# A recurrence's step products in one TensorE form, and its score loads by halves in other gaps

## The chip, the cores and the metric

One core of a Trainium2 chip runs the whole kernel as one program. The metric is the device time of one execution in microseconds (us). PE is TensorE (matrix products, with PEld for its weight loads), DVE is VectorE, ACT is ScalarE, POOL is GpSimd and SP is SyncE, which only issues DMAs here.

## The reference

A decoder trunk of two layers over 16 meta tokens and 1024 tokens of width 1024. The first layer mixes by the RWKV-7 recurrence, the second by stick-breaking attention; each is followed by a conv-gated MLP. The change lies in the first layer's recurrence alone:

```
def step(S, inp):                       # per head, S is 64 x 64, 16 heads, 1040 tokens
    r_t, w_t, k_t, v_t, a_t, b_t = inp  # a_t = -kk, b_t = kk * a, w_t = decay
    sa = jnp.einsum('bhij,bhj->bhi', S, a_t)
    S = (S * w_t[:, :, None, :] + sa[..., None] * b_t[:, :, None, :]
         + v_t[..., None] * k_t[:, :, None, :])
    return S, jnp.einsum('bhij,bhj->bhi', S, r_t)
_, y = lax.scan(step, S0, seq)
...                                     # then a group norm of y per head, a bonus, a gate and w_o
```

## The kernel before

The projections of the first layer are written to DRAM per segment of 512 tokens (two segments, s) and per four heads (four groups, q), scaled by the running products of the decay. `rwkv_chain` then runs the recurrence in chunks of 64 tokens. A unit is one (q, s): four heads, as two pairs u with two heads e each, over eight chunks. There are eight units, one after the other; before them stands a prelude that loads and prepares the first ones and does the 16 meta tokens (`first_chunk`).

`stage_c` is the serial part. For each chunk c (a step) it makes c1 = AR x S0 (tile c), adds KV and gets R (on DVE), makes c2 = XT x R (tiles c and c2b), copies it to UV (DVE and ACT), makes c3 = BKt x UV (tile c again) and from it the next state S, and makes the output yp from UV x Ar and S0 x AR. Between these products stand three gaps per step, 24 in a unit. I call gap c.k the gap behind the first (k = 0), second (1) and last products (2) of step c. What fills a gap is written out by hand in the table `SEQ`, one string of letters per gap. Each letter pulls a generator one step:

- A (`stage_a`, two units ahead): loads BK and AR, then makes the scores A, which go masked to Aa, and writes them to DRAM as AD. B (`stage_b`): the second half of the scores, Ar.
- L and S (`stage_s`, two units ahead) and s (one unit ahead): load AT, which is AD spread to four copies, 1 MB; copy XL; then 31 steps of forward substitution, two POOL instructions each (prd = AT x XL, XL += prd); at the end XL is written to DRAM as XD.
- x and X (`stage_x`, one ahead): load X11t from XD, transpose it on DVE to X, and make XT by two rounds of small products G.
- V, T (one ahead): v and BK transposed by TensorE (vt, kv, bt). F (one back): the norm of y: products hr_gn and hp_gn, on POOL y x G and later y + B, then the store of y to DRAM.

`PRE` is the like table of the prelude. The engines DVE, POOL and SP run these instructions in the order in which they are written (`InOrder`), TensorE as well (`pmm`). So a wait of one instruction holds all that are behind it on its engine, and a DMA that waits on SP holds the DMAs behind it.

AR is zero in the rows of the other head: AR[es, u, e] is loaded for es alone and the rest is cleared once. UV and BKt are laid out by head in the same way. In the form names of the profile, 128*64 is a product with 128 rows of contraction and 64 columns of weights, 64*64 one with 64 and 64.

Of the kernel before, what the change touches and what calls it, by code (L numbers as in the profile page):

```python
# [9 lines left out]
F32 = mybir.dt.float32  # L10
F32R = mybir.dt.float32r
AF = mybir.ActivationFunctionType
ALU = mybir.AluOpType
# [3 lines left out]
P = 128  # L17
# [34 lines left out]
def kernel(ctx: ExitStack, tc: tile.TileContext, a: dict, out: bass.AP):  # L52
# [142 lines left out]
    NC = 8  # L195
# [586 lines left out]
    def rwkv_chain(late, early, last):  # L782
# [13 lines left out]
        def pmm(*args, **kw):  # L796
            return tc.keep_in_program_order(mm(*args, **kw))  # L797

        def ptr(*args):
# [8 lines left out]
            g=16, S=128, R=128, PS=128, y=1024, GB=1024, ysq=1024, XT=1024, Ar=2048, UV=2048, BKt=2048, KV=1024, AR=4096,  # L808
# [21 lines left out]
        selw = rp.tile([P, 64], F32, name="selw")  # L830
# [54 lines left out]
        def norm_out(nm, y, nt, per, G1, B1, dst):  # L885
# [8 lines left out]
            for i in range(nt):  # L894
                pmm(ps[:, 64 * i : 64 * i + 64], ysq[:, i * P : (i + 1) * P], selw, start=True, stop=True)
                if i == 3:
                    yield
# [3 lines left out]
                xs.rearrange("p (i e) -> p i e", e=2), ps.rearrange("p (i x) -> p i x", x=64)[:, 0:nt, 0:2],  # L901
# [190 lines left out]
        def stage_a(q, s, ed):  # L1092
            nm = f"{q}{s}"
            AR = ARs[(4 * s + q) % 3]
            BK = [place(f"BK{'ab'[u]}{q % 2}", f"BK{u}_{nm}") for u in range(2)]
            for u in range(2):
                LQ.dma_start(BK[u], BK_s[s][q][:, u, 0:1024])
                for e in range(2):
                    es = slice(64 * e, 64 * e + 64)
                    LQ.dma_start(AR[es, u, e, :], AR_s[s][q][es, u, 0:1024])  # L1100
            ed.update(AR=AR, BK=BK)
            yield
            Aa = place(f"Aa{q % 2}", f"Aa{nm}").rearrange("p (u c e t) -> p u c e t", u=2, c=NC, e=2)
            ed["Aa"] = Aa

            AD = dr.tile([4, NC, 32, 2, 32], F32, tag="AD", bufs=2, name=f"AD{nm}")
            for u in range(2):
                yield from chunk_mats(nm, BK, AR, 0, Aa, u)
                flush(evacs)
                for b4 in range(4):  # L1110
                    e, b = b4 // 2, b4 % 2
                    LQ.dma_start(
                        AD[b4][:, :, u, :].rearrange("c j t -> j c t"),
                        Aa[32 * b4 : 32 * b4 + 32, u, :, e, 32 * b : 32 * b + 32],
                    )
            ed["AD"] = AD
            yield

        def stage_s(q, s, ed):
            nm = f"{q}{s}"  # L1120
            AD = ed["AD"]
            AT = place(f"AT{q % 2}", f"AT{nm}").rearrange("p (j u t) -> p j u t", j=32, u=2)
            LQ.dma_start(
                AT.rearrange("p j u t -> p (j u t)"),
                AD.rearrange("q c j u t -> (q c) (j u t)").unsqueeze(0).broadcast_to([4, 32, 2048]),
            )
            yield
# [112 lines left out]
        def stage_c(q, s, ed, gap):  # L1240
# [3 lines left out]
            for c in range(NC):  # L1244
# [3 lines left out]
                R = place(f"R{c % 2}", f"R{nm}{c}").rearrange("p (u d) -> p u d", u=2)  # L1248
                PS0 = place(f"PS{c % 2}", f"PS{nm}{c}").rearrange("p (u d) -> p u d", u=2)
                c1 = ps_c(f"c1{nm}{c}")  # L1250
                for u in range(2):
                    for e in range(2):
                        es = slice(64 * e, 64 * e + 64)
                        pmm(c1[es, u * 64 : u * 64 + 64], arv[es, u, e, c, 0, :], S0[es, u, :], start=True, stop=True)
                gap()
                V.tensor_tensor(R, c1[:, 0:128].rearrange("p (u d) -> p u d", u=2), KV[:, :, c, :], op=ALU.add)
# [4 lines left out]
                for u in range(2):  # L1261
                    for e in range(2):
                        us = slice(64 * e, 64 * e + 64)
                        pmm(c2[e][us, u * 64 : u * 64 + 64], XT[us, u, c, :], R[us, u, :], start=True, stop=True)
# [10 lines left out]
                yp = ps_y(f"yp{nm}{c}")  # L1275
                for u in range(2):
                    for e in range(2):
                        es = slice(64 * e, 64 * e + 64)
                        o = slice(u * 64, u * 64 + 64)
                        pmm(yp[es, o], UV[:, u, c, e, :], Ar[:, u, c, e, :], start=True, stop=False)  # L1280
                        pmm(yp[es, o], S0[es, u, :], arv[es, u, e, c, 1, :], start=False, stop=True)
# [37 lines left out]
        def gens(fn):  # L1319
# [6 lines left out]
            "A": (gA, 2), "B": (gB, 1), "L": (gS, 2), "S": (gS, 2), "s": (gS, 1), "x": (gX, 1), "X": (gX, 1),  # L1326
            "V": (gV, 1), "T": (gT, 1), "F": (gF, -1),
        }
        before = {"L": gA, "x": gS}
# [10 lines left out]
        def run(gs):  # L1340
# [6 lines left out]
            "a W2 f c2 a11 s2 A b20 a9 f v s4 t5 A t15 s2 A s2 A2 s2 A s2 A s6 A s2 A2 s2 A A s4 A s2 "  # L1347
            "A2 s A s2 A s9 A2 s2 A13 s2 A2 s4 S2 v20 f34 s30 x21 S20 W3 f "
# [3 lines left out]
            "TFAsTsss VFTTsssss Asss AFTssss AFAFssss AAssss FBsss FAssss AFss AFV LxBB V BF VF V VF SV "  # L1352
            "VBSSS VBSBSSF VBSS SXSVXBS XSSSXF XSSSS BXSSSXSFF "
# [9 lines left out]
        def clear_rest():  # L1363
            for t in ARs[1:]:
                clear(t, G)
            yield
            for t in XTs:
                G.memset(t, 0.0)
            yield
# [4 lines left out]
            "c": clear_rest(),  # L1374
# [1155 lines left out]
```

## Time and profile before

| what | value |
|---|---|
| device time, median of three runs | 3647.41 us (3642.76 to 3652.55) |
| the profiled execution's own time | 3653.89 us |
| its span, first to last instruction | 3652.2 us |
| PE busy | 3205.0 us (88%) |
| DVE, ACT, POOL busy | 2310.3, 1558.4, 1737.8 us |
| mean granted TensorE clock | 0.914 of full |

The span is what the profile covers; the time beside it also holds what lies around the first and the last instruction. A busy share is a mean over stages with different limits: the recurrence is about one seventh of the span, and only its own stretch tells what bounds it. The granted clock has two levels, 1.00 (2.4 GHz) and 0.50 (1.2 GHz). A row of the windows' view holds the stretch (us from the span's start), its length, the busy time of PE, PEld, DVE, ACT and POOL with their instructions, the granted clock, the DMA engines' busy share and GB/s. A timeline row holds the start, the time taken, engine, line, operation, output and inputs, form and count.

### The profile page before, as it was taken

The numbers are of one execution on the slowest core, as the hardware profiler recorded it, in microseconds if no ns is written. First come the engines' busy times: TensorE is split into PE (matmuls) and PEld (weight loads), VectorE is DVE, ScalarE is ACT, GpSimd is POOL, SyncE is SP. The second block draws the span as 40 slices with busy tenths as digits, with TensorE's granted clock in tenths as the row PEclk, the third lists the DMA queues.
The fourth block names the chain that finished last, engine by engine and source line by source line (L and its number), as shares of the span: only waits on it lengthen the run. The fifth ranks groups of instructions, "written<-read, shape, count | busy, mean of one in ns | idle before, by whom it ended". The sixth has DMA issues, their size and how long they took to land.

```text
span 3652.2 us, 62577 instructions
## 1 busy us (share of the span) xinstructions
PE 3205.0 (88%) x25101; PEld 2967.3 (81%) x25101; DVE 2310.3 (63%) x3064; ACT 1558.4 (43%) x2859; POOL 1737.8 (48%) x1676
## 2 busy tenths in 40 slices
PE   4798688489889979999999988888888699998998
PEld 4796466367777969999899978788878699998998
DVE  8778866423232488888734377777774888887342
ACT  4664544133344333333323266666653333334232
POOL 5555634343644465445422366666644544444221
PEclk7898799679887989999999999999999799999999
DMA  6344343443434422222445301010025222224453
GB/s 200 109 152 132 122 129 113 117 100 85 118 94 148 132 63 76 76 82 73 145 140 164 98 22 29 24 33 24 21 100 165 94 78 80 76 79 139 122 165 95
DMA packets 438398, 366.61 MB, mean 100 GB/s; under 512 B 66823, under 2 KB 359453, under 8 KB 436827
## 3 DMA queue, kind: packets, MB, share of 16 engines
q1 hardware_dynamic: 437243, 361.28, 32.8%
q8 instruction: 197, 3.23, 0.4%
q0 software_dynamic: 864, 1.33, 0.1%
q14 instruction: 94, 0.77, 0.1%
HBM read 266.51 MB, written 96.02 MB: 99 GB/s over the span
## 4 chain that ended last, share of the span: by engine, by line
PE 48%; DVE 20%; DMA 7%; ACT 6%; issue 5%; POOL 4%; SPq 1%; ACTq 0%; DVEq 0%; POOLq 0%
PE dn L1508 12%; DVE t L1691 5%; DMA XD<-XL 3%; PE yp L797 3%; PE kps L2090 2%; DVE rs L1616 2%; DVE om L2245 2%; PE c L797 1%; PE wt L2093 1%; ACT t L1689 1%; PE wo L1900 1%; PE vps L2090 1%; PE kp L217 1%; DMA araw<-a_s 1%; PE av L2090 1%
## 5 line engine op out<-in xcount | busy, mean ns | idle before, releaser
L1508 PE MATMUL dn<-act,h_dn 128*128 128x260 f32 x2688 | 437.0, 284 | 5.0 <-ACT act L76 3.3
L1508 PEld LDWEIGHTS dn<-act,h_dn 128*128 128x128 f32 x2688 | 373.2, 190 | 5.8 <-ACT act L76 3.7
L1691 DVE SCALAR_TENSOR_TENSOR t<-u,pcol,t 128x1040 f32<-128x1040 f32 x168 | 304.1, 1811 | 108.7 <-ACT t L1689 108.6
L1508 PE MATMUL dn<-act,l_dn 128*128 128x260 f32 x1344 | 273.2, 285 | 2.0 <-POOL l_dn L1457 2.0
L2248 POOL TENSOR_TENSOR be<-be,om 128x911 f32<-128x911 f32 (+7 forms) x128 | 195.7, 1529 | 130.4 <-DVE om L2245 103.6
L1457 POOL TENSOR_TENSOR l_dn<-r_dn,h_dn 128x1024 fp32r<-128x1024 f32 (+1 forms) x46 | 101.6, 2208 | 325.0 <-ACT h_dn L76 324.2
L2245 DVE TENSOR_TENSOR_SCAN om<-om 128x912 f32<-128x912 f32 (+7 forms) x128 | 215.7, 1685 | 48.2 <-POOL om L2240 30.1
L1706 POOL TENSOR_TENSOR t<-t,t 128x1040 f32<-128x1040 f32 x42 | 103.3, 2460 | 250.5 <-DVE t L1691 250.5
L76 ACT ACTIVATE h_dn<-r_dn 128x1024 fp32r<-128x1024 f32 (+1 forms) x92 | 90.7, 986 | 298.5 <-PE dn L1508 272.9
L1508 PEld LDWEIGHTS dn<-act,l_dn 128*128 128x128 f32 x1344 | 207.1, 189 | 2.4 <-POOL l_dn L1457 2.4
L44 POOL TENSOR_TENSOR prd<-AT,XL 128x108 f32<-128x108 f32 (+24 forms) x217 | 80.4, 371 | 164.5 <-DMA AT<-AD 111.6
L1457 POOL TENSOR_TENSOR s34l<-rs,s34h 128x1024 fp32r<-128x1024 f32 x44 | 105.8, 2405 | 103.2 <-ACT s34h L76 103.2
L76 ACT ACTIVATE WT<-wt 128x512 fp32r<-128x512 f32 (+2 forms) x224 | 98.7, 443 | 120.3 <-PE wt L2093 92.0
L2311 DVE TENSOR_TENSOR WT<-wt,WT 128x512 fp32r<-128x512 f32 (+2 forms) x224 | 107.6, 488 | 53.2 <-ACT WT L76 49.4
L2090 PE MATMUL av<-WT,VS 128*128 128x256 f32 (+3 forms) x640 | 108.4, 283 | 32.6 <-DVE WT L2311 32.5
L76 ACT ACTIVATE s34h<-rs 128x1024 fp32r<-128x1024 f32 x44 | 46.7, 1062 | 202.8 <-PE wo L1508 5.1
L1457 DVE TENSOR_TENSOR l_dn<-r_dn,h_dn 128x1024 fp32r<-128x1024 f32 (+1 forms) x46 | 52.0, 1131 | 123.1 <-ACT h_dn L76 123.0
L2093 PE MATMUL wt<-ident,be 128*128 128x128 f32 x576 | 99.3, 295 | 34.4 <-DVE WTm L2286 33.6
L217 PE MATMUL kp<-xm,wh_rw_wk 128*128 128x264 f32 (+1 forms) x384 | 108.3, 375 | 17.6 <-DVE xm L396 10.5
L2240 POOL TENSOR_SCALAR_AFFINE_SELECT be<-be 128x128 f32<-128x128 f32 x128 | 78.6, 614 | 91.9 <-ACT be L2235 91.9
L2090 PEld LDWEIGHTS av<-WT,VS 128*64 128x64 f32 (+1 forms) x640 | 85.5, 165 | 43.7 <-DVE WT L2311 42.5
L797 PE MATMUL A<-ARz,BK 128*128 128x128 f32 x512 | 86.7, 311 | 30.7 <-DVE prd L44 20.5
(2104 smaller groups left out, 11207.5 us busy)
## 6 DMA issues: line engine op xcount, KB each, us to landing
r_dn<-in_ffn_down_dram SPq DMA_DIRECT2D x60, 512.0 KB
a_s<-t SPq DMA_DIRECT2D x84, 260.0 KB
rv<-in_ffn_up_dram SPq DMA_DIRECT2D x42, 512.0 KB
ra<-in_ffn_up_dram SPq DMA_DIRECT2D x42, 512.0 KB
araw<-a_s SPq DMA_DIRECT2D x50, 260.0 KB
r_dn<-in_ffn_down_dram SPq DMA_DIRECT2D x32, 384.0 KB
raw<-a_s SPq DMA_DIRECT2D x36, 260.0 KB
hr<-h_s SPq DMA_DIRECT2D x32, 260.0 KB
```

Source lines behind the costliest of these rows:

```text
L76: return S.activation(o, i, AF.Copy, scale=scale)
L217: return tc.keep_in_program_order(mm(*args, **kw))
L797: return tc.keep_in_program_order(mm(*args, **kw))
L1457: eng.tensor_tensor(lo, x, f(hi), op=ALU.subtract)
L1508: self.mm(ps[:, c, :], w[:, kk, :], X[k][i][:, c * CH : (c + 1) * CH], start=k == 0 and j == 0, stop=k == len(X) - 1 and j == 2,)
L1691: VV.scalar_tensor_tensor(t[j], u[j][:, i : i + n], w, t[j], op0=ALU.mult, op1=ALU.add)
L1706: (G if n == L else VV).tensor_tensor(t[1], t[0], t[1], op=ALU.mult)
L2090: return tc.keep_in_program_order(mm(*args, **kw))
L2093: return tc.keep_in_program_order(nc.tensor.transpose(*args))
L2245: V.tensor_tensor_scan(om[0:nq, 0:nk], om[0:nq, 0:nk], om[0:nq, 0:nk], 1.0, op0=ALU.mult, op1=ALU.min)
L2248: G.tensor_tensor(be[0:nq, 1:nk], be[0:nq, 1:nk], om[0:nq, 0 : nk - 1], op=ALU.mult)
L2311: V.tensor_tensor(wt[:, 1, s0:s1], ps[:, s0:s1], f(wt[:, 0, s0:s1]), op=ALU.subtract)
```

## The change

The products c1, c2 and the second half of yp take all 128 rows instead of the 64 of their own head; for this R gets a zeroed place for the other head (`Rs`, cleared once on POOL), and its addition becomes two instructions, one per head. In yp the two heads' products follow each other, first UV x Ar for both, then S0 x AR for both. The constant selw of the norm is half as wide. `stage_a` yields between the loads of BK and of AR, writes AD by pair u, and loads AT by halves itself, one half behind each pair's scores. `stage_s` loads nothing any more. The tables put the letters into other gaps, L is gone, and a new letter P pulls `stage_a` three units ahead (its first step, the loads of BK).

```
-        selw = rp.tile([P, 64], F32, name="selw")
+        Rs = [place(f"R{i}", f"Rz{i}").rearrange("p (u e d) -> p u e d", u=2, e=2) for i in range(2)]
+
+        selw = rp.tile([P, 32], F32, name="selw")
...
             for u in range(2):
                 LQ.dma_start(BK[u], BK_s[s][q][:, u, 0:1024])
+            yield
+            for u in range(2):
                 for e in range(2):
                     es = slice(64 * e, 64 * e + 64)
                     LQ.dma_start(AR[es, u, e, :], AR_s[s][q][es, u, 0:1024])
...
-            AD = dr.tile([4, NC, 32, 2, 32], F32, tag="AD", bufs=2, name=f"AD{nm}")
+            AD = dr.tile([2, 4, NC, 32, 32], F32, tag="AD", bufs=2, name=f"AD{nm}")
+            AT = ed["AT"] = place(f"AT{q % 2}", f"AT{nm}").rearrange("p (u j t) -> p u j t", j=32, u=2)
             for u in range(2):
                 yield from chunk_mats(nm, BK, AR, 0, Aa, u)
                 flush(evacs)
                 for b4 in range(4):
                     e, b = b4 // 2, b4 % 2
                     LQ.dma_start(
-                        AD[b4][:, :, u, :].rearrange("c j t -> j c t"),
+                        AD[u][b4].rearrange("c j t -> j c t"),
                         Aa[32 * b4 : 32 * b4 + 32, u, :, e, 32 * b : 32 * b + 32],
                     )
-            ed["AD"] = AD
+                LQ.dma_start(
+                    AT[:, u].rearrange("p j t -> p (j t)"),
+                    AD[u].rearrange("q c j t -> (q c) (j t)").unsqueeze(0).broadcast_to([4, 32, 1024]),
+                )
             yield
 
         def stage_s(q, s, ed):
             nm = f"{q}{s}"
-            AD = ed["AD"]
-            AT = place(f"AT{q % 2}", f"AT{nm}").rearrange("p (j u t) -> p j u t", j=32, u=2)
-            LQ.dma_start(
-                AT.rearrange("p j u t -> p (j u t)"),
-                AD.rearrange("q c j u t -> (q c) (j u t)").unsqueeze(0).broadcast_to([4, 32, 2048]),
-            )
-            yield
+            AT = ed["AT"].rearrange("p u j t -> p j u t")
...
-                        pmm(c1[es, u * 64 : u * 64 + 64], arv[es, u, e, c, 0, :], S0[es, u, :], start=True, stop=True)
+                        pmm(c1[es, u * 64 : u * 64 + 64], arv[:, u, e, c, 0, :], S0[:, u, :], start=True, stop=True)
                 gap()
-                V.tensor_tensor(R, c1[:, 0:128].rearrange("p (u d) -> p u d", u=2), KV[:, :, c, :], op=ALU.add)
+                for e in range(2):
+                    es = slice(64 * e, 64 * e + 64)
+                    V.tensor_tensor(
+                        R[es, :, e, :], c1[es, 0:128].rearrange("p (u d) -> p u d", u=2), KV[es, :, c, :], op=ALU.add
+                    )
...
-                        pmm(c2[e][us, u * 64 : u * 64 + 64], XT[us, u, c, :], R[us, u, :], start=True, stop=True)
+                        pmm(c2[e][us, u * 64 : u * 64 + 64], XT[:, u, c, :], R[:, u, e, :], start=True, stop=True)
...
                 for u in range(2):
+                    o = slice(u * 64, u * 64 + 64)
                     for e in range(2):
-                        es = slice(64 * e, 64 * e + 64)
-                        o = slice(u * 64, u * 64 + 64)
-                        pmm(yp[es, o], UV[:, u, c, e, :], Ar[:, u, c, e, :], start=True, stop=False)
-                        pmm(yp[es, o], S0[es, u, :], arv[es, u, e, c, 1, :], start=False, stop=True)
+                        pmm(yp[64 * e : 64 * e + 64, o], UV[:, u, c, e, :], Ar[:, u, c, e, :], start=True, stop=False)
+                    for e in range(2):
+                        pmm(yp[64 * e : 64 * e + 64, o], S0[:, u, :], arv[:, u, e, c, 1, :], start=False, stop=True)
...
         SEQ = (
-            "TFAsTsss VFTTsssss Asss AFTssss AFAFssss AAssss FBsss FAssss AFss AFV LxBB V BF VF V VF SV "
-            "VBSSS VBSBSSF VBSS SXSVXBS XSSSXF XSSSS BXSSSXSFF "
+            "ATsss TVsss TTsss AAsss AAsss AAsss AAsss Asss FBsss BBsss xFV BFV "
+            "BFVS BFVSSS BFVSSS BFVSSS BFVSSS XVFSSS XFSSS XFSSS XFSSS XFSSS XFPSSS XFFSSSS "
         ).split()
```

On TensorE, this is the second half of a step in unit 3 of eight, before: c from UV and BKt is the last state product, yp the first half of the output group (its second half repeats it), in turn from Ar and UV and from AR and the state S.

```order
L797 MATMUL c_8498<-UV_7958,BKt_7716 64x64 x4
L797 MATMUL yp_8503<-Ar_7892,UV_7958 64x64
L797 MATMUL yp_8503<-ARz_5796,S_8445 64x64
L797 MATMUL yp_8503<-Ar_7892,UV_7958 64x64
L797 MATMUL yp_8503<-ARz_5796,S_8445 64x64
```

The same place of the changed kernel, with the scores A that follow in the gap:

```order
L797 MATMUL c_8494<-UV_7980,BKt_7743 64x64 x4
L797 MATMUL yp_8499<-Ar_7930,UV_7980 64x64 x2
L797 MATMUL yp_8499<-ARz_5796,S_8451 64x64 x2
L797 MATMUL yp_8499<-Ar_7930,UV_7980 64x64 x2
L797 MATMUL yp_8499<-ARz_5796,S_8451 64x64 x2
L797 MATMUL A_8513<-ARz_5798,BK_11_8345 128x128 x4
```

The eight products are the same in number; they now stand in pairs of one kind.

On SP, this is one unit's round of DMAs before, from the store of the unit's predecessor's y (y_s) to the loads of X11t; G, B and vc are inputs of the norm and of V.

```order
L44 DMA y_s_91<-y_6421 128x512
L44 DMA G_7722<-g_s_138 128x2x512
L44 DMA BK_01_7724<-BK_s_125 128x1024
L44 DMA ARz_5797<-AR_s_117 64x1024 x2
L44 DMA BK_01_7725<-BK_s_125 128x1024
L44 DMA ARz_5797<-AR_s_117 64x1024 x2
L44 DMA vc_7751<-vc_s_132 128x2x512
L44 DMA B_7756<-b_s_146 128x2x512
L44 DMA AD_7792<-Aa_7791 32x8x32 x8
L44 DMA AT_7974<-AD_7792 128x1x2048
L44 DMA XD_7983<-XL_7470 256x1x64 x4
L44 DMA X11t_7988<-XD_7983 32x8x64 x4
```

The same round of the changed kernel:

```order
L44 DMA y_s_91<-y_6435 128x512
L44 DMA BK_01_7697<-BK_s_125 128x1024
L44 DMA BK_01_7698<-BK_s_125 128x1024
L44 DMA ARz_5797<-AR_s_117 64x1024 x4
L44 DMA vc_7768<-vc_s_132 128x2x512
L44 DMA AD_7815<-Aa_7814 32x8x32 x4
L44 DMA AT_7816<-AD_7815 128x1x1024
L44 DMA AD_7815<-Aa_7814 32x8x32 x4
L44 DMA AT_7816<-AD_7815 128x1x1024
L44 DMA G_7928<-g_s_138 128x2x512
L44 DMA XD_7953<-XL_7395 256x1x64 x4
L44 DMA X11t_7969<-XD_7953 32x8x64 x4
```

AT goes out in two halves, the first between the two groups of AD writes; G and B (behind X11t) have moved back, and the store of y still stands ahead of BK and AR.

On POOL, this is where y + B stands in the substitution of one unit, before; the last number of a row counts down from 31 with the steps of the substitution.

```order
L44 TENSOR_TENSOR XL_8116<-XL_8116,prd_8155 128x4x26
L44 TENSOR_TENSOR prd_8155<-AT_7974,XL_8116 128x4x25
L44 TENSOR_TENSOR XL_8116<-XL_8116,prd_8155 128x4x25
L44 TENSOR_TENSOR y_7062<-y_7062,B_7756 128x1024
L44 TENSOR_TENSOR prd_8155<-AT_7974,XL_8116 128x4x24
```

And in the changed kernel:

```order
L44 TENSOR_TENSOR XL_8042<-XL_8042,prd_8066 128x8x19
L44 TENSOR_TENSOR prd_8066<-AT_7816,XL_8042 128x8x18
L44 TENSOR_TENSOR y_7085<-y_7085,B_7978 128x1024
L44 TENSOR_TENSOR XL_8042<-XL_8042,prd_8066 128x8x18
L44 TENSOR_TENSOR prd_8066<-AT_7816,XL_8042 128x8x17
```

It has moved from behind the fourteenth instruction of the substitution to behind the twenty-seventh.

## Rows read from the trace of the kernel before

**Rows 1.** The page's head.

```profile
span 3652.2 us, 62577 instructions
```

**Rows 2.** Windows: units 0, 6, 7, the sum of all eight, and within unit 7.

```profile
755.60:811.20 55.60, 48.92 (x613) 39.22 (x614) 15.42 (x49) 21.02 (x57) 25.42 (x67) 0.84 0.33 81
...
1099.90:1145.60 45.70, 44.52 (x608) 35.67 (x608) 13.85 (x45) 22.54 (x59) 18.39 (x39) 0.91 0.23 64
1145.60:1203.00 57.40, 53.99 (x405) 43.45 (x406) 14.23 (x43) 19.87 (x49) 20.59 (x13) 0.62 0.65 200
sum 447.40, PE 407.25 PEld 328.49 DVE 126.79 ACT 175.99 POOL 204.87; mean PE 50.91 PEld 41.06 DVE 15.85 ACT 22.00 POOL 25.61
...
1146.00:1184.00 38.00, 36.25 (x252) 29.20 (x254) 8.83 (x28) 15.28 (x36) 18.24 (x12) 0.50 0.76 236
```

**Rows 3.** Windows inside unit 3.

```profile
928.10:931.90 3.80, 3.80 (x22) 3.07 (x23) 0.57 (x2) 2.38 (x6) 3.56 (x5) 0.50 1.04 268
931.90:970.30 38.40, 37.90 (x444) 30.56 (x442) 13.42 (x40) 13.21 (x39) 12.34 (x33) 1.00 0.29 73
970.30:975.80 5.50, 0.02 (x1) 0.00 (x0) 0.75 (x2) 1.35 (x3) 4.38 (x14) 0.73 0.22 52
975.80:986.20 10.40, 10.01 (x177) 8.26 (x178) 1.99 (x8) 5.57 (x13) 7.83 (x15) 0.50 0.58 180
```

**Rows 4.** Waits of PE from 755 to 1146 us: total, times, longest.

```profile
PE G L797 <- DVE X L44: 30.6, 6, 6.0
```

**Rows 5.** Timeline of SP in unit 3: start, us, what.

```profile
951.65 0.57 SPq L44 DMA_DIRECT2D AT<-AD  x1
952.26 4.66 SPq L44 DMA_DIRECT2D XD<-XL  x4
971.37 2.03 SPq L44 DMA_DIRECT2D X11t<-XD  x4
979.17 0.81 SPq L44 DMA_DIRECT2D y_s<-y  x2
```

**Rows 6.** Timeline of POOL in unit 3; in brackets the idle time before.

```profile
970.41 0.29 POOL L44 TENSOR_TENSOR prd<-AT,XL 128x62 f32<-128x62 f32 x1 [23.66 <-DMA AT<-AD]
...
976.80 2.35 POOL L44 TENSOR_TENSOR y<-y,B 128x1024 f32<-128x1024 f32 x1 [0.78 <-DVE y L44]
```

**Rows 7.** Window while AT is under way.

```profile
955.00:970.30 15.30, 15.19 (x215) 12.19 (x213) 5.20 (x14) 5.25 (x15) 0.00 (x0) 1.00 0.28 71
```

**Rows 8.** Timeline of PE at the end of a step in unit 3.

```profile
939.39 0.45 PE L797 MATMUL c<-UV,BKt 128*64 128x64 f32 x8
939.67 0.28 PE L797 MATMUL yp<-Ar,UV 128*64 128x64 f32 x2
...
941.67 1.16 PE L797 MATMUL A<-ARz,BK 128*128 128x128 f32 x8
942.76 0.45 PE L797 MATMUL c<-S,ARz 64*64 64x64 f32 x8
943.14 0.71 PE L797 MATMUL A<-ARz,BK 128*128 128x128 f32 x4
```

**Rows 9.** Tile R's addition (min/median/max ns), and two S instructions from DVE's timeline.

```profile
L44 DVE TENSOR_TENSOR R<-c,KV x64: 278/291/293, 755.6 to 1197.0; 128x128 f32<-128x128 f32 x64
940.18 0.47 DVE L44 SCALAR_TENSOR_TENSOR S<-c,PC,PS 128x64 f32<-128x64 f32 x2
```

**Rows 10.** Timeline of PE: the first A product of a unit.

```profile
934.53 0.71 PE L797 MATMUL A<-ARz,BK 128*128 128x128 f32 x4
```

**Rows 11.** Timeline of PE: a step in unit 7.

```profile
1159.29 0.73 PE L797 MATMUL c<-S,ARz 64*64 64x64 f32 x7
...
1161.95 0.42 PE L797 MATMUL yp<-Ar,UV 128*64 128x64 f32 x2
...
1164.89 0.73 PE L797 MATMUL c<-S,ARz 64*64 64x64 f32 x7
```

**Rows 12.** The chain of waits in the prelude: start, us, what.

```profile
678.53 23.03 DMA AT<-AD
```

More of the change, by code (lines that the diff above doesn't have):

```diff
@@ L807, in rwkv_chain @@
         size = dict(
-            g=16, S=128, R=128, PS=128, y=1024, GB=1024, ysq=1024, XT=1024, Ar=2048, UV=2048, BKt=2048, KV=1024, AR=4096,
+            g=16, S=128, R=256, PS=128, y=1024, GB=1024, ysq=1024, XT=1024, Ar=2048, UV=2048, BKt=2048, KV=1024, AR=4096,
             BKa=1024, BKb=1024, Aa=2048, AT=2048, XL=512, prd=512, vc=1024, xx=512,
@@ L894, in norm_out @@
             for i in range(nt):
-                pmm(ps[:, 64 * i : 64 * i + 64], ysq[:, i * P : (i + 1) * P], selw, start=True, stop=True)
+                pmm(ps[:, 32 * i : 32 * i + 32], ysq[:, i * P : (i + 1) * P], selw, start=True, stop=True)
                 if i == 3:
@@ L900, in norm_out @@
             later.append(lambda: V.tensor_scalar(
-                xs.rearrange("p (i e) -> p i e", e=2), ps.rearrange("p (i x) -> p i x", x=64)[:, 0:nt, 0:2],
+                xs.rearrange("p (i e) -> p i e", e=2), ps.rearrange("p (i x) -> p i x", x=32)[:, 0:nt, 0:2],
                 1.0 / 64, GN_EPS, op0=ALU.mult, op1=ALU.add,
@@ L1247, in stage_c @@
                 S0 = state[q]
-                R = place(f"R{c % 2}", f"R{nm}{c}").rearrange("p (u d) -> p u d", u=2)
+                R = Rs[c % 2]
                 PS0 = place(f"PS{c % 2}", f"PS{nm}{c}").rearrange("p (u d) -> p u d", u=2)
@@ L1325, in rwkv_chain @@
         by = {
-            "A": (gA, 2), "B": (gB, 1), "L": (gS, 2), "S": (gS, 2), "s": (gS, 1), "x": (gX, 1), "X": (gX, 1),
-            "V": (gV, 1), "T": (gT, 1), "F": (gF, -1),
+            "A": (gA, 2), "B": (gB, 1), "S": (gS, 2), "s": (gS, 1), "x": (gX, 1), "X": (gX, 1),
+            "V": (gV, 1), "T": (gT, 1), "F": (gF, -1), "P": (gA, 3),
         }
-        before = {"L": gA, "x": gS}
+        before = {"S": gA, "x": gS}
         def pull(code, i):
@@ L1346, in rwkv_chain @@
         PRE = (
-            "a W2 f c2 a11 s2 A b20 a9 f v s4 t5 A t15 s2 A s2 A2 s2 A s2 A s6 A s2 A2 s2 A A s4 A s2 "
-            "A2 s A s2 A s9 A2 s2 A13 s2 A2 s4 S2 v20 f34 s30 x21 S20 W3 f "
+            "a2 W2 f c2 a11 s2 A2 b20 a9 f v s4 t5 A t15 s2 A s2 A2 s2 A s2 A s6 A s2 A2 s2 A A s4 A s2 "
+            "A2 s A s2 A s9 A2 s2 A13 s2 A2 s4 S1 v20 f34 s30 x21 p2 S20 W3 f "
         ).split()
@@ L1365, in clear_rest @@
                 clear(t, G)
+            for t in Rs:
+                G.memset(t, 0.0)
             yield
@@ L1373, in rwkv_chain @@
             "a": gA[0], "A": gA[1], "s": gS[0], "S": gS[1], "t": gT[0], "b": gB[0], "v": gV[0], "x": gX[0], "f": fc,
-            "c": clear_rest(),
+            "c": clear_rest(), "p": gA[2],
         }
```

## The prediction

> **What bounds the kernel now.** The page was read first: the profiled execution spans 3652.2 us [rows 1] and took 3653.9 us, 6.5 above the median of the three timed runs, 3647.4. The change touches only the recurrence, which runs from about 658 us (its loads) to 1203 us. I then cut this stretch at the first R addition of each of its eight units. Units 0 to 7 take 55.6, five times 57.7 on the average (447.4 less the three others, over five), 45.7 and 57.4 us [rows 2]. In all of them TensorE is busy for some nine tenths, so I looked at where a unit loses the rest and what clock it has.
>
> Within unit 3 [rows 3] there are 38.4 us at a granted clock of 1.00 (2.4 GHz) with TensorE almost without a gap, then 5.5 us in which it does nothing, then a stretch at 0.50 (1.2 GHz), which reaches into the next unit: 10.4 us and, as at this unit's own start, another 3.8, so about 14.1. So the work of a unit at the full clock is 38.4 + 14.1/2 = 45.4 us. The rest of the 58 is the stall and the slow clock behind it. The stall is product G waiting for the transposed X [rows 4], about 5 us in each of units 0 to 5 (30.6 us in six waits).
>
> Why X is late stands in SP's queue and POOL's row. The load of AT is issued at 951.65, the writes of XD right behind it, and the loads of X11t only at 971.37 [rows 5], since SP holds them until XD has landed. POOL waits 23.66 us for the same AT and starts its substitution at 970.41 [rows 6]. So one 1 MB load takes 18.8 us, while the DMA engines are 0.28 busy [rows 7], some four and a half of sixteen. What is queued behind it on those few engines waits along.
>
> **The products over 128 rows.** Now four products c of form 128*64 take 0.28 us from their start to the first yp, while the yp group takes 2.00 us (939.67 to 941.67) for twice as many [rows 8]: it changes between forms 128*64 and 64*64 seven times. After the change all eight have one form and alternate in column halves as the four c do. At c's pace they take 0.56; I leave 0.10 for the change of form into what follows, which is what the 64*64 group c<-S shows over 0.28 (942.76 to 943.14). The gain is 2.00 - 0.56 - 0.10 = 1.34 us a step at the full clock, 10.7 a unit, and the unit's TensorE work falls from 45.4 to 34.7 us.
>
> The c<-S and c<-R groups go from 64*64 to 128*64. Rows 8 has both forms for equally many columns: 0.38 with a change of form behind it, 0.28 without. I cost this at nothing. The Trainium skill says the opposite in "TensorEngine Tiling (Array Packing)", section Theoretical Speedup: a contraction of up to 64 rows may gain up to 2x by row tiling, which the change gives up. By it c<-S, c<-R and the S half of yp would each cost 0.28 us more, 0.84 a step or 54 us over 64 steps, and leave 0.50 of the 1.34. The rows speak for the first reading, because the code pairs row half e with column half e alone, so two such products run side by side in either form.
>
> R is written by two additions instead of one. One takes 0.29 us, and a pair of S instructions 0.47 together [rows 9], so the second adds about 0.2 to the way from c<-S to c<-R. Behind most first gaps that is hidden by the gap's products (at least 0.85 us); where a gap is empty or short it shows. I count 3 us a unit for this and the like (one empty second gap, the wait for GT). Nothing is gained or lost by the narrower selw, whose 128*128 weights still have to be loaded. TensorE alone would then allow 34.7 + 3 = 38 us a unit, and 40 with a few us of slow clock.
>
> **The moved loads.** Gap c.k is the gap k of step c. A's products now stand in gaps 1.0 to 2.0, and the two AT halves are issued after each half. Substitution starts at 4.0 instead of 5.1 and X at 5.2 instead of 6.2. This should take the AT load out of XD's way, but it closes a loop from unit to unit, which I follow from the first A product in gap 1.0 (time 0). A's sixteen products, at 1.09 us for four (941.67 to 942.76 [rows 8]) plus the step's own, end at 5.7. With evacuation (0.7) and four AD writes the second half of AT is issued at about 11 and the first at 7.5. At the pace of today's load both have landed at 7.5 + 18.8 = 26.3; if the halves move at twice that pace, at 11 + 9.4 = 20.4. I take 23.5. POOL then does 27 instructions (the 28 S codes ahead of gap 7.1's F, less the copy): 14 took 5.6 us before the stop at 976.02 [rows 6] and the later ones are longer, together 12.1. Behind them in POOL's order is y + B, 2.35, with its gap 2.4. Only then can SP store y, and behind that store on SP stand the loads of BK and AR for the next A products. So they are issued at 23.5 + 12.1 + 2.4 = 38.0.
>
> The store and the BK and AR rows that the first A product needs are 2 MB. At the 180 GB/s of the stretch that has such loads [rows 3] that is 11.5 us. Bounds: from the y store at 979.17 [rows 5] to the first A product 13.4 us later (934.53 plus a period of 58.1 [rows 10]) nothing waited, which is the upper one; at the 268 GB/s that the engines reach when full [rows 3] 7.8. So the next A can start at 49.5, bounds 20.4 + 14.5 + 7.8 = 42.7 and 26.3 + 14.5 + 13.4 = 54.2. TensorE is there at 38 and waits, in gap 1.0, for BK and AR. XD, too, is issued right behind the second half of AT, so a part of the G wait may stay. I take 49 us.
>
> The loop needs a predecessor. Unit 2's BK and AR are loaded by the prelude, and unit 3's in unit 0, behind a small first chunk's y. So units 0 and 1 miss the wait for A: I take 45 and 44 for them (38, some of the G wait, slow clock).
>
> Unit 6 has no A and no AT: its 45.7 us lose the yp gain of 10.7 and become 35. Unit 7 runs its first half at 1.2 GHz [rows 2], with steps like the one from 1159.29 to 1164.89 [rows 11], 5.6 us, where yp takes 2.94 (1161.95 to 1164.89). A yp of 1.0 leaves the chain of R, UV and S, about 4.1 us. Four such steps and a smaller gain in the four that hold wo products: 11 us. In the prelude, AT takes 23.03 us from its issue [rows 12]; a half sent earlier may save 0 to 10, and I take 5.
>
> **Sum.** Prelude 5, unit 0 55.6 - 45 = 11, unit 1 57.7 - 44 = 14, units 2 to 5 4 x (57.7 - 49) = 35, unit 6 11, unit 7 11: 87 us. The profiled execution would take 3653.9 - 87 = 3567, and 3647.4 - 87 gives 3560 us.
>
> **Rivals.** (1) *No loop:* TensorE bounds, 40 us in units 0 to 5. For it: if the AT halves land by 20 and the loads are quick, the stall is small, and the clock stays up. Against: even with POOL in time, y + B cannot start before gap 7.1, and from there to gap 1.0 there are five gaps, about 8 us at 38/24 each, for 2.4 + 7.8. Gain 344.3 - 240 = 104, with the other 27 131 us: 3516 us. The Trainium skill bears on it in "DMA: Bandwidth & Descriptors", section on why a DMA increments its semaphore by 16: an outermost dimension of four copies confines a DMA to four engines. By that rule, the trace agrees with its 0.28 [rows 7], the halves stay as confined as the whole; spread over sixteen they would land by about 13 and this rival would win.
>
> (2) *Given back:* the waits for A and G both stay, each brings the slow clock as the G stall does now, and units 0 to 5 come to 55: gain 14 + 27 = 41, 3606 us.
>
> (3) *Slower:* the clock stays at 1.2 GHz for most of a unit, since TensorE has more gaps. A unit of 34.7 us of work plus 3 is as long as today's 57.7 when 40 us of it run at half clock (34.7 + 3 + 40/2); above that it is slower, and wholly at half clock it takes 72. For it: unit 7 is at 0.50 for 38 us of mostly step products [rows 2]. Against: the 38.4 us at 1.00, which hold as many of them [rows 3]. With seven units at 72: about 100 us more, 3750 us.
>
> (4) *No effect:* the substitution chain sets the period as before, and what yp saves becomes waiting: 3647 us.
>
> **Chances.** The loop 0.50, no loop 0.25, given back 0.14, slower 0.07, no effect 0.04. A measurement of this kernel tells about 0.3% (11 us) from no change; so faster 0.89, within 0.04, slower 0.07. The loop's own range is 3531 to 3590 (its bounds on four units, and 8 for the rest). To leave out no more than two in ten the range goes from 3495, past most of the no-loop case, to 3612, past the middle of the given-back one.
>
> **What would show it.** In the profile after: the yp group at about 0.6 us and one form; c<-S no longer than now; PE waits for ARz or BK in front of A, 8 to 11 us in units 2 to 5, and SP's y store just before them, released by POOL; POOL's wait for AT still there; the G wait below 5 us; a yp-free step chain of 4 us in unit 7. The prediction is wrong if A never waits (then 3516 or less), if c<-S or c<-R doubles, or if the clock row of a unit shows more than 40 us at 0.50.

## The result and the profile after

The changed kernel takes 3627.56 us (median of six runs, 3625.98 to 3631.33) against 3652.7 for the kernel before, run beside it: ratio 0.9935, 95% interval 0.9918 to 0.9952. It is 0.65% faster: some 25 us between the medians, not 87; forecast were 3560 us and a range that ended at 3612. The profiled execution spans 3626.7 us, 25.5 less than before [rows 1].

The windows' view of the kernel after, cut as in [rows 2]: one row for each of units 0 to 7, then the sum.

```profile
755.70:808.30 52.60, 39.66 (x613) 34.04 (x614) 17.96 (x57) 20.50 (x57) 19.11 (x53) 0.76 0.27 60
808.30:860.90 52.60, 42.87 (x641) 36.77 (x642) 18.80 (x59) 21.77 (x59) 25.97 (x61) 0.79 0.35 86
860.90:921.70 60.80, 43.78 (x641) 37.65 (x642) 18.88 (x58) 21.94 (x59) 27.93 (x65) 0.75 0.40 101
921.70:978.70 57.00, 43.24 (x641) 37.16 (x642) 18.86 (x58) 21.76 (x59) 27.02 (x63) 0.80 0.39 108
978.70:1040.40 61.70, 44.31 (x641) 38.26 (x642) 19.00 (x59) 22.10 (x59) 29.00 (x67) 0.75 0.38 100
1040.40:1102.10 61.70, 45.85 (x641) 39.41 (x642) 18.88 (x58) 21.87 (x59) 27.96 (x65) 0.75 0.38 99
1102.10:1141.40 39.30, 35.71 (x608) 29.98 (x608) 16.00 (x54) 21.72 (x59) 16.86 (x36) 0.88 0.30 89
1141.40:1187.90 46.50, 36.13 (x407) 31.12 (x408) 17.61 (x51) 20.36 (x49) 21.28 (x15) 0.74 0.80 246
sum 432.20, PE 331.55 PEld 284.38 DVE 145.99 ACT 172.02 POOL 195.12; mean PE 41.44 PEld 35.55 DVE 18.25 ACT 21.50 POOL 24.39
```

TensorE is busy 331.55 us in the eight units, 75.7 less than before, yet the units together are only 15.2 us shorter. Units 0, 1, 6 and 7 gained; units 2 to 5, at 57.6 each before on the average, now take 60.3. Inside unit 4 the windows show where:

```profile
...
985.30:995.50 10.20, 5.61 (x42) 5.07 (x44) 1.78 (x4) 0.27 (x1) 7.99 (x24) 0.50 0.65 153
995.50:1013.00 17.50, 16.91 (x238) 14.52 (x236) 8.56 (x26) 7.07 (x24) 0.00 (x0) 1.00 0.33 73
1013.00:1019.40 6.40, 3.10 (x80) 2.67 (x80) 1.65 (x7) 0.87 (x2) 0.00 (x0) 1.00 0.54 132
1019.40:1025.60 6.20, 0.00 (x0) 0.00 (x0) 1.07 (x3) 1.92 (x4) 4.86 (x10) 0.50 0.43 121
1025.60:1040.40 14.80, 14.76 (x233) 12.89 (x234) 3.95 (x13) 7.64 (x20) 10.41 (x22) 0.50 0.02 7
```

There are two stalls of TensorE where there was one. Within each the granted clock falls to 0.50 (1.2 GHz) and stays there when TensorE works again: 10.2 us, and then 21.0 of this unit. TensorE is busy for 20.4 us of these two stretches (5.61 and 14.76); before it was 13.8 a unit [rows 3]. The timeline of PE names the two stalls: the idle time and its releaser stand in brackets.

```profile
989.89 2.05 PE L797 MATMUL A<-ARz,BK 128*128 128x128 f32 x8 [7.06 <-DMA ARz<-AR_s]
...
1010.06 0.29 PE L797 MATMUL yp<-Ar,UV 128*64 128x64 f32 x4
...
1010.63 0.71 PE L797 MATMUL A<-ARz,BK 128*128 128x128 f32 x4
...
1011.88 0.45 PE L797 MATMUL c<-S,ARz 128*64 128x64 f32 x8
1012.26 0.71 PE L797 MATMUL A<-ARz,BK 128*128 128x128 f32 x4
...
1025.64 0.69 PE L797 MATMUL c<-S,ARz 128*64 128x64 f32 x8 [9.54 <-DVE S L44]
```

The yp group takes 0.57 us (1010.06 to 1010.63) where it took 2.00 [rows 8], and c<-S takes the same 0.38 to the next product as in its 64*64 form. So the products did what was forecast. The second stall is new in kind: a step's c waits for S, which VectorE has not made. VectorE's timeline says why:

```profile
1012.38 0.61 DVE L44 TENSOR_TENSOR Rz<-c,KV 64x128 f32<-64x128 f32 x2 [1.55 <-PE c L797]
...
1024.43 0.71 DVE L44 STREAM_TRANSPOSE X<-X11t 128x512 f32<-128x512 f32 x1 [9.66 <-DMA X11t<-XD]
1025.06 0.43 DVE L44 SCALAR_TENSOR_TENSOR S<-c,PC,PS 128x64 f32<-128x64 f32 x2
```

The transposition that makes X is pulled in gap 5.2, and the code of a gap stands ahead of the step's S. It waits 9.66 us for X11t, and S, ready otherwise, waits in line. Units 1 to 5 all have this stall (7.8 to 10.4 us); in unit 0 the same late X11t holds ScalarE, and TensorE stands 10.6 us in front of hp_gn. Why X11t is late, and A too, is read from SP's timeline through one period:

```profile
979.24 1.62 SPq L44 DMA_DIRECT2D y_s<-y  x2
...
981.93 2.78 SPq L44 DMA_DIRECT2D ARz<-AR_s  x4
...
995.33 1.81 SPq L44 DMA_DIRECT2D AD<-Aa  x4
998.47 0.57 SPq L44 DMA_DIRECT2D AT<-AD  x1
999.18 2.57 SPq L44 DMA_DIRECT2D AD<-Aa  x4
1008.39 0.55 SPq L44 DMA_DIRECT2D AT<-AD  x1
1008.99 0.56 SPq L44 DMA_DIRECT2D G<-g_s  x1
1009.60 3.73 SPq L44 DMA_DIRECT2D XD<-XL  x4
1020.87 1.80 SPq L44 DMA_DIRECT2D X11t<-XD  x4
...
1039.85 0.81 SPq L44 DMA_DIRECT2D y_s<-y  x2
```

After the second AD writes (last issued by 1001.75) SP stands until 1008.39, when they have landed and it may send the second AT half. The first half is then on the same queues. The packets show what it does to the writes behind it. AD's are of 128 bytes, and in the middle of this wait, from 1002.6 to 1006.1, the DMA view has no packet under 512 bytes:

```profile
DMA packets 70, 0.30 MB, mean 85 GB/s; under 512 B 0, under 2 KB 0, under 8 KB 69
```

Told apart by their sizes, 768 of the 1024 packets of the second AD writes are through by 1002.58. The other 256, a quarter, move from 1006.13, as the first half (999.83 to 1007.02) ends, to 1007.64. A quarter of XD's and of G's packets is held in the same way behind the second half (1009.73 to 1017.68): their last ones end at 1020.46 and 1019.53. So SP waits for XD until 1020.87, and POOL, whose order has y x G right ahead of the substitution's first step, waits for G:

```profile
1020.11 2.34 POOL L44 TENSOR_TENSOR y<-y,G 128x1024 f32<-128x1024 f32 x1 [25.02 <-issue]
...
1037.47 2.36 POOL L44 TENSOR_TENSOR y<-y,B 128x1024 f32<-128x1024 f32 x1 [2.90 <-DVE y L44]
```

In this unit the profile names no releaser for y x G ("issue"), in units 1 and 2 it names G. The y + B behind the substitution waits once more, for VectorE's y.

### The profile page after: what moved, and what is told of

The parts are those of the page before. It is cut to its first block, busy times and chain, and to the rows that moved or that the text cites. A ratio compares the mean times of both kernels' runs of the same rounds, so it can differ in the third digit from the quotient of the medians.

```text
span 3626.7 us, 62709 instructions
## 1 busy us (share of the span) xinstructions
PE 3120.0 (86%) x25101; PEld 2913.6 (80%) x25101; DVE 2329.0 (64%) x3128; ACT 1554.7 (43%) x2859; POOL 1735.9 (48%) x1678
## 4 chain that ended last, share of the span: by engine, by line
PE 45%; DVE 20%; DMA 9%; ACT 6%; issue 5%; POOL 4%; SPq 2%; ACTq 0%; DVEq 0%; POOLq 0%
PE dn L1517 12%; DVE t L1700 5%; DVE om L2254 2%; PE kps L2099 2%; DVE rs L1625 2%; DMA AD<-Aa 2%; PE c L797 1%; POOL be L2257 1%; SPq L44 1%; ACT t L1698 1%; PE wt L2102 1%; PE kp L217 1%; DMA XD<-XL 1%; PE av L2099 1%; PE A L797 1%
## 5 line engine op out<-in xcount | busy, mean ns | idle before, releaser
L2320 DVE TENSOR_TENSOR WT<-wt,WT 128x512 fp32r<-128x512 f32 (+2 forms) x224 | 107.6, 488 | 51.6 <-ACT WT L76 48.2
L797 PEld LDWEIGHTS A<-ARz,BK 128*128 128x128 f32 x512 | 75.6, 224 | 65.2 <-issue 34.8
L217 PE MATMUL kp<-xm,wh_rw_wk 128*128 128x264 f32 (+1 forms) x384 | 109.0, 376 | 19.1 <-DVE xm L396 10.5
```

What stands on the lines that cost most here:

```text
L2320: V.tensor_tensor(wt[:, 1, s0:s1], ps[:, s0:s1], f(wt[:, 0, s0:s1]), op=ALU.subtract)
```

## Experiments

Unit lengths are windows cut as above; "before" and "changed kernel" are the two kernels of the case. Lines of PE's waits hold the total, the number and the longest, from 750 to 1200 us.

**1. Products alone**, on the kernel before (with the narrower selw, for room):

```diff
-pmm(c1[es, ...], arv[es, u, e, c, 0, :], S0[es, u, :], ...)
+pmm(c1[es, ...], arv[:, u, e, c, 0, :], S0[:, u, :], ...)
-V.tensor_tensor(R, c1[...], KV[:, :, c, :], op=ALU.add)
+for e in range(2):
+    V.tensor_tensor(R[es, :, e, :], c1[es, ...], KV[es, :, c, :], op=ALU.add)
...
```

> The kernel before with the product part of the change alone: 128 contraction rows, R zero-padded and written by two additions, the eight yp products of a half in turn, selw narrowed to make room. The tables of gaps, the AT load as one and the loads of BK and AR stay as before. Theory (the products gain what was forecast, and the new order of the gaps gives it back): yp 2.00 -> about 0.6 us; unit 6 shorter by some 8 to 11 us and unit 7 by about 10, as in the changed kernel; units 0 to 5 shorter by 3 to 8 us each, the rest of the 10.7 turning into a longer wait of G for X, since the chain AT, substitution, XD, X11t is as long as before. Sum 40 to 65 us, ratio to before 0.982 to 0.989, so faster than the whole change (0.9935). Rival (the products bring little by themselves, their gain is the R addition, waits and clock eating it at once): ratio 0.995 to 1.000.

Ratio 0.985 (0.9833 to 0.9867): 55 us, more than twice the whole change. Units 6 and 7 are 38.2 and 43.3 us (7.5 and 14.1 shorter than before, where 8 to 11 and about 10 were expected), units 1 to 5 52.1 on the average. The wait of G, 30.6 us in six before [rows 4], is now

```profile
PE G L797 <- DVE X L44: 58.1, 7, 11.2
```

so nearly half of what yp saves in a unit turns into waiting for X.

**2. The new order and loads alone**: the changed kernel with the products of before, the reverse of the diff above.

> The changed kernel with the products of before (64 contraction rows, one R addition, yp products changing form seven times), so the tables of gaps and the loads by halves alone. Theory (the new order loses): A waits for ARz and c for S as in the changed kernel, since the way from A over AT and the substitution to the store of y sets the period; units 2 to 5 at 60 to 64 us, unit 6 at 46 and unit 7 at 51 to 55; ratio to before 1.000 to 1.010. Rival (the order is harmless, the waits come only because the faster steps reach A and S earlier): units at 55 to 57, ratio 0.985 to 0.997.

Ratio 1.0099 (1.0083 to 1.0115). Units 2 to 5 take 63.2 us, units 0 and 1 58.1 and 61.7, units 6 and 7 48.1 and 59.6. The two halves of the change multiply to 0.985 x 1.0099 = 0.9948, near the 0.9935 of the whole: in the total they hardly act on each other. Two parts of the expectation failed. A doesn't wait here, and c waits only 3.1 to 4.0 us for S in units 2 to 5; units 6 and 7 are longer than expected, and than before. The loss goes with the clock: it is 0.74 in each of units 2 to 5, where before it was 0.85 or 0.86. This is the short stall of unit 3 and what follows:

```profile
982.60:985.40 2.80, 0.19 (x8) 0.06 (x2) 0.00 (x0) 0.63 (x1) 2.17 (x9) 0.89 0.33 76
985.40:1016.10 30.70, 29.31 (x298) 23.55 (x300) 5.76 (x18) 13.37 (x30) 21.05 (x47) 0.51 0.42 120
```

**3. X later**: the changed kernel with the X letters from gap 6.2 on.

```diff
-"BFVS BFVSSS BFVSSS BFVSSS BFVSSS XVFSSS XFSSS XFSSS XFSSS XFSSS XFPSSS XFFSSSS "
+"BFVS BFVSSS BFVSSS BFVSSS BFVSSS VFSSS FSSS FSSS XXFSSS XXFSSS XFPSSS XXFFSSSS "
```

> The changed kernel with the seven X letters pulled in gaps 6.2 to 7.2 (as many there as in the kernel before), not from 5.2 on, so that the transposition of X stands on VectorE behind the S instructions of steps 5 and 6.0. Nothing else is changed. Theory (X waits ahead of S): the wait of c for S of about 10 us in step 5 goes; steps 5 and 6 run on while XD lands, and G waits 1 to 4 us. But the substitution on GpSimd ends only some 3 us before the y product it waits for, so y's store and the next A move by little: units 2 to 5 shorter by 2 to 6 us each, units 0 and 1 by 4 to 9; ratio to before 0.983 to 0.990. Rival (clock): the stall goes and the slow stretch behind it goes with it, units 0 to 5 to about 49, ratio 0.975 to 0.980. Rival (the order on VectorE is not it, X is late for all): the wait moves whole to G, ratio 0.992 to 0.995.

Ratio 0.9908 (0.989 to 0.9925), just past the first theory. Units 2 to 5 come to 57.3. The wait for S has gone, and most of it is G's again, 5.1 to 7.2 us in units 1 to 5 where 1 to 4 were expected; A waits as long as ever:

```profile
PE G L797 <- DVE X L44: 35.9, 7, 7.2
PE A L797 <- DMA ARz<-AR_s: 27.7, 4, 7.7
```

VectorE's order made the stall 8 to 10 us where it now is 5 to 7. X itself is late. In this run y + B waits for nothing in units 1 to 5: the substitution ahead of it on POOL is what ends last there, and the period from A to A is still 58.3 us (984.43 to 1042.68).

**4. AT over more engines**: the changed kernel, each half in four transfers.

```diff
-LQ.dma_start(AT[:, u]..., AD[u].rearrange("q c j t -> (q c) (j t)").unsqueeze(0).broadcast_to([4, 32, 1024]))
+for g in range(4):
+    LQ.dma_start(AT[32 * g : 32 * g + 32, u]..., AD[u].rearrange("q c j t -> (q c) (j t)"))
```

> The changed kernel with each AT half loaded by four transfers of 32 partitions each, in place of one transfer whose first dimension is the four copies. Bytes are the same; SP issues eight transfers in place of two. Theory (a load confined to some four and a half of the sixteen engines holds AD's second writes, G, XD and X11t): the share of busy DMA engines behind the AT issue goes from about 0.3 to above 0.6, a half lands in 2 to 4 us in place of 7 to 10, the second half is issued some 5 us earlier, X11t lands 8 to 12 us earlier, and the wait of c for S in step 5 goes below 2 us; the wait of A for ARz goes to 0 to 4 us. Units 2 to 5 to 47 to 52 us, ratio to before 0.970 to 0.983. Rival (the loop is SP's order and GpSimd's substitution, the engines matter little): units stay at 58 to 61, ratio 0.990 to 0.996.

Ratio 0.9752 (0.9734 to 0.9769). SP's timeline in its unit 4:

```profile
943.53 3.16 SPq L44 DMA_DIRECT2D AT<-AD  x4
946.74 1.90 SPq L44 DMA_DIRECT2D AD<-Aa  x4
949.92 2.68 SPq L44 DMA_DIRECT2D AT<-AD  x4
...
953.25 2.61 SPq L44 DMA_DIRECT2D XD<-XL  x4
958.32 2.48 SPq L44 DMA_DIRECT2D X11t<-XD  x4
```

From the second AD writes to the second AT half are 3.2 us in place of 9.2, from XD to X11t 5.1 in place of 11.3. The windows' view, first of the changed kernel behind its first half, then of this one behind its two, gives the share of busy DMA engines (last but one number):

```profile
998.50:1008.40 9.90, 9.31 (x130) 8.00 (x130) 4.95 (x14) 3.67 (x12) 0.00 (x0) 1.00 0.28 70
```

```profile
943.50:950.00 6.50, 5.91 (x94) 5.11 (x90) 3.45 (x11) 2.91 (x10) 0.00 (x0) 1.00 0.43 103
950.00:957.40 7.40, 7.40 (x104) 6.35 (x104) 3.05 (x10) 3.30 (x11) 0.00 (x0) 1.00 0.66 178
```

The waits for S fall from 47.1 us to 10.8, none over 2.5. The prelude gains as well: the first R addition comes at 733.9, not 755.7. But units 2 to 5 only come to 52.3, because A still waits, against what was expected:

```profile
PE A L797 <- DMA ARz<-AR_s: 31.0, 4, 9.7
```

**5. and 6. The same edit in the order of before**, to its one AT load: without the products, then with them (runs 1 and 4 joined).

> The kernel before with one thing changed: its one AT load of 1 MB is issued as four transfers of 32 partitions each, in place of one whose first dimension is the four copies. Theory (a load confined to some four and a half engines holds XD and X11t, and this makes the wait of G in both kernels): AT lands 10 to 15 us earlier, the prelude is shorter by about 20 us as in the changed kernel with the same edit, the wait of G for X (30.6 us in six) goes below 6, and units 0 to 5 come to 49 to 53 us. Ratio to before 0.977 to 0.987. Rival (in this order the load is long hidden, and the substitution on GpSimd sets X): only the prelude gains, ratio 0.992 to 0.995.

Ratio 0.9847 (0.9834 to 0.986). In unit 3, to be held against [rows 5]:

```profile
906.98 1.71 SPq L44 DMA_DIRECT2D AT<-AD  x4
...
916.14 2.11 SPq L44 DMA_DIRECT2D X11t<-XD  x4
```

From AT's issue to X11t's are 9.2 us in place of 19.7. G no longer waits for X in units 0 to 5, which take 47.9 us (unit 0) and 51.6 on the average (1 to 5).

> The kernel before with the product part of the change and with the AT load issued as four transfers; order of the gaps and loads as before. Theory: the two gains add, since the waits of G for X in the products-alone run (58.1 us in seven) come from the same load. TensorE then sets the unit: 40 to 44 us in units 0 to 5 against 49 to 53 with the products alone, prelude shorter by about 20; ratio to before 0.960 to 0.970, faster than the changed kernel with the same edit (0.975). Rival (the next limit, GpSimd's substitution or the loads of BK and AR, stands close behind): units 46 to 50, ratio 0.972 to 0.978.

Ratio 0.9649 (0.9636 to 0.9663), 3522 us: the gains add (0.985 x 0.9847 = 0.9699, and more, since the 58.1 us that G waited in run 1 fall to 4.7). Units 0 to 4 take 40.1 to 43.7 us, as expected; unit 5, at 48.2, doesn't. One of them:

```profile
855.60:898.20 42.60, 39.60 (x641) 33.83 (x642) 19.30 (x58) 22.18 (x59) 27.76 (x64) 0.90 0.53 139
```

**7. and 9. BK ahead of y's store**: the letter P in gap 6.0 in place of 7.1, with run 4's AT edit (7) and without it (9).

```diff
-... XVFSSS XFSSS XFSSS XFSSS XFSSS XFPSSS XFFSSSS "
+... XVFSSS PXFSSS XFSSS XFSSS XFSSS XFSSS XFFSSSS "
```

> The changed kernel with AT by four transfers a half, and with the BK loads (letter P) pulled in gap 6.0 in place of 7.1, that is on SP ahead of y's store. In the run with the AT edit alone A waited 8 to 10 us for ARz in units 2 to 5, with y's store (0.5 MB), BK (1 MB) and AR (1 MB) issued together at the end of the unit. Theory (the first A waits for the bytes that are queued together): BK's 1 MB moves out of that burst, 3.7 us at 268 GB/s, so the wait of A falls by 2.5 to 4 us, and units 2 to 5 from 51 to 54 us to 47 to 51; ratio to before 0.969 to 0.973 against 0.975. Rival (A waits for the AR issue itself, which stands behind the unit's last products): nothing changes, 0.974 to 0.977.

Ratio 0.9682 (0.9669 to 0.9694); units 2 to 5 come to 47.0 from 52.3, at the good end of the first theory and in the ratio a little past it.

> The changed kernel with the BK loads (letter P) pulled in gap 6.0 in place of 7.1, and nothing else: AT still in two halves of one transfer each. It undoes a part of the loop from y's store to A, and leaves the late AT. Theory (the loop and the late AT each hold a part): A waits for ARz 2.5 to 4 us less in units 2 to 5, from 24.3 in four to 8 to 15; c still waits some 8 to 10 us for S in step 5 of each unit; units 2 to 5 shorter by 2 to 4 us, ratio to before 0.987 to 0.991 (changed kernel 0.9935). Rival (the late AT alone sets the period, and A's wait only absorbs it): the wait goes over to S, ratio 0.992 to 0.995. Rival (the loop alone): units 2 to 5 shorter by 6 to 10 us, ratio 0.98 to 0.985.

Ratio 0.9852 (0.9835 to 0.9868), more than expected; units 2 to 5 come to 54.9 from 60.3, and PE's waits are

```profile
PE c L797 <- DVE S L44: 48.7, 12, 9.7
...
PE A L797 <- issue: 7.4, 3, 3.4
...
PE A L797 <- DMA ARz<-AR_s: 4.8, 1, 4.8
```

A still stands in each of the four units, in three of them with no releaser that the profile shows ("issue"): 12.2 us together, half of the changed kernel's 24.3, as expected. The wait for S stands untouched. So the two stalls are two causes. From y's store to the first A of unit 4 are now 6.3 us (974.05 to 980.31) in place of 10.65: 4.4 less, near the 3.7 that I had counted for BK's 1 MB at 268 GB/s. The units gain more than A's wait loses (5.4 us against 3.0); their clock is 0.76 to 0.84, the changed kernel's 0.75 to 0.80.

**8. The order of the yp products**: run 1 with UV and S product of one column half behind each other again, all over 128 rows.

> The products-alone kernel with the eight yp products in the order of before (UV and S product of one column half, then of the other), all still over 128 rows. It parts the yp gain into the form (no change between 64 and 128 rows) and the order (column halves in turn). If the form makes it: yp 0.6 to 0.7 us, ratio to before as with the products alone, 0.985. If the order makes part of it, because two products on the same column half don't run beside each other: yp 0.9 to 1.2 us, 2 to 5 us a unit back in units 6 and 7, partly hidden in units 0 to 5 by the wait of G; ratio 0.986 to 0.990. If the order makes all: yp near 2.0 and ratio 0.995 to 1.000.

Ratio 0.9837 (0.9823 to 0.9851), unit 6 at 38.3 us as in run 1. The yp group is as fast as with the halves in turn:

```profile
980.04 0.33 PE L797 MATMUL yp<-Ar,UV 128*64 128x64 f32 x4
...
980.65 0.63 PE L800 MATMUL vt<-ident,vc 128*64 128x128 f32 x4
```

0.61 us. The one form makes the gain; the order adds nothing.

**10. All three waits of the changed kernel treated**: AT by four transfers, P in gap 6.0, X from gap 6.0 on.

> The changed kernel with its three waits treated at once: AT halves by four transfers each, BK loads in gap 6.0, the X letters from gap 6.0 on in place of 5.2. The run with the first two gave 0.9682, with 12.5 us of waits for S left and units 2 to 5 at 44 to 52. Theory: the waits for S go below 4 us, units 0 to 5 come to 42 to 46, near the order of before with products and AT by four transfers (40 to 48); ratio to before 0.961 to 0.966. Rival (X is late by itself, not VectorE's order): G waits instead, 0.967 to 0.970.

Ratio 0.9636 (0.9622 to 0.9651), 3522 us. The waits for S fall to 1.7 us. Units 0 to 5 spread more than expected, from 40.3 to 50.7 us, with 45.2 on the average. The new order can be as good as the old one, and the intervals of this run and run 6 overlap. Unit 4, the shortest, shows what the forecast had called TensorE alone, 40 us:

```profile
915.00:955.30 40.30, 36.47 (x641) 31.09 (x642) 19.41 (x59) 21.86 (x59) 25.66 (x63) 0.98 0.57 152
```

## Why the prediction was wrong

**The products: right.** yp measured 0.57 us, forecast 0.66; c<-S unchanged at 0.38, forecast to cost nothing; unit 7 46.5 us, as forecast, with a step of 3.97 in its slow half (1149.76 to 1153.73), forecast 4. The Trainium skill ("TensorEngine Tiling (Array Packing)", Theoretical Speedup) gives up to 2x for tiling a contraction of up to 64 rows; the trace doesn't bear it out for c<-S, whose 64-row form was no faster. The second R addition adds 0.32 us a step (0.61 for the two, at 1012.38 in VectorE's timeline above, against the 0.29 of [rows 9]), where I had 0.2. Unit 6 came to 39.3, not 35: its clock is 0.88, and TensorE is busy 35.71 us. TensorE alone at 38 to 40 us a unit is borne out as a floor only: the shortest of units 0 to 5 take 40.1 (run 6) and 40.3 (run 10), their averages are 43.3 and 45.2.

**The loop: it is there, but three of its steps were wrong.** A waits for ARz in units 2 to 5 and not in 0 and 1, behind y's store, 4.8 to 7.3 us where 8 to 11 were forecast. From that store to the first A product are 10.65 us (979.24 to 989.89), forecast 11.5. But the period from first A to first A is 60.4 us (989.89 to 1050.29), forecast 49.5: y's store is issued 50.0 us behind the first A (989.89 to 1039.85), not 38.0. The 12 us that are missing lie in three places.

- The first is "four AD writes the second half of AT is issued at about 11": it is issued at 18.5 (989.89 to 1008.39). Of these 7.5 us, 1.1 lie ahead of the first half (8.6, not 7.5). The other 6.4 are nearly all the second AD writes, which I let pass freely beside the first half: 6.6 us pass from their last issue to the second half, in run 4, where AT isn't confined, 1.3. I had weighed the halves' own pace (9.4 or 18.8 us), and not what a half already under way does to the small writes on which the next half depends. The second half itself then takes 9.3 us, less than I had allowed, so AT is there at 27.8, not 23.5 (bounds 20.4 and 26.3): 4.3 of the 12.
- "POOL then does 27 instructions" takes 12.15 us (1022.41 to 1034.56), forecast 12.1. But y x G stands ahead of them on POOL, waits for G behind the second half, and takes 2.34 us. I had put this at nothing; it costs 4.7. So POOL still waits, as forecast, but for G, not AT.
- y + B then waits 2.9 us more (2.2 to 2.9 in units 1 to 5) for VectorE's y, which comes from products that TensorE makes behind its stall at S. So the last to release y's store is TensorE's chain, not the substitution. Without that stall, in run 3, the path is the one that I forecast, with y x G in it, and even so has a period of 58.3 us.

The Trainium skill ("DMA: Bandwidth & Descriptors", on why a DMA increments its semaphore by 16) has the number of engines of a transfer be the largest, up to 16, that divides the slowest dimension (of those that aren't 1) of both its patterns: four copies, four engines. The share of 0.28, run 4's higher ones and the quarter of AD's, XD's and G's packets that is held agree.

**The wait for X: sized at "a part", in the wrong place.** I had XD right behind the second half, and still took 49 us. XD goes out 19.7 us after the first A and X11t 31.0 after it (1020.87). And I had looked for the wait at G, where TensorE would stand with its S made. By moving X to gap 5.2 the change put the transposition ahead of S on VectorE, which stops the recurrence itself: 9.5 us in unit 4, 46.0 in units 1 to 5. Run 3 puts 3.0 us of each of units 2 to 5 to VectorE's order; run 4, with 10.8 us of waits for S left in all, puts most of the stall to the late AT.

**The sum.** Before, in the same cut, unit 1 took 58.2 us and units 2 to 5 together 230.5. Units 2 to 5 were to give 35 us and cost 10.7 (57.0 + 60.8 + 2 x 61.7 = 241.2); units 0 and 1 gave 8.6, not 25; unit 6 6.4, not 11; unit 7 10.9, as forecast; the prelude 0, not 5. The nearest rival is *given back*, which I had at 0.14: two waits, each with slow clock, though the second is at S and not at G. Its 55 a unit should have been 57.7 (units 0 to 5 take 346.4). The range had its middle in it and no more, so it ended below the result. So the recurrence gave 15 us of the 87. The remaining 10.4 of the 25.5 us lie behind it (2449.2 us before, 2438.8 after). That part takes between 2438.8 and 2455.5 in all twelve profiles, without following any edit; I don't put it to the change.

**The other rivals.** *No loop* would have come with AT "spread over sixteen", I wrote. Run 4 does that and the loop's wait of A stays, so that condition was wrong. It bears out what I had put against this rival: y + B can't start before gap 7.1, and the transfers behind it (10.5 us from y's store to A, 976.19 to 986.71) are longer than the gaps that are left. It takes BK's bytes out of the burst as well (run 7), and X off S (run 10). Run 10's 3522 us then are near what the rival said (3516), in part by luck: its six units take 45.2 us, not 40, and its prelude gave 24 us (731.2 for 755.6), not 5. *Slower by clock* didn't come for the changed kernel; run 2, without the yp gain, is slower and at a clock of 0.74, about half of each unit at 0.50.

**What stays open.** Why the clock needs 30.7 us to return in run 2, and 14.1 in the kernel before after a longer stall; and what the units of run 10 above 40 us wait for, one by one.

## What to carry to other kernels

A gain on the bounding engine is worth what the next chain of transfers allows: follow that chain with its small dependent writes, since these waited here behind a large transfer that kept about a quarter of the engines busy, and price each at the landing, not at the issue. When a waiting instruction is moved earlier on an in-order engine, look at what stands behind it there; the same lateness cost 3.0 us a unit more in front of the recurrence than in front of a filler product (run 3). And split a change into its halves on the chip early: here one half gave 1.5% and the other took 1.0%, and a third edit of a few lines, which neither had, gave 1.5% by itself.

## What the runs showed of the hardware that was not expected

A stall of 4.0 us can cost more clock than one of 5.5 [rows 3]: behind it, in run 2, TensorE was at 0.51 for 30.7 us while busy 29.31 of them. A load whose first dimension is its four copies held a quarter of each transfer behind it: 256 of AD's 1024 packets move 3.5 us behind the others, as the AT half ahead of them ends (1002.58 to 1006.13). Four DMA starts in place of one cost SP 1.1 us (1.71 for 0.57) and brought 10.5 us on the way from AT to X11t (19.7 to 9.2). Eight products of one form cost the same whether two behind each other write the same column half or not (0.61 and 0.57 us).
